# Twenty pieces of modulation weights, loaded from ScalarE's queue in place of SyncE's

## The chip, the core and the metric

The kernel runs on one core of a Trainium2 chip. A core has five engines that work side by side: TensorE (PE, matrix products into PSUM; its weight loads are shown apart as PEld), VectorE (DVE), ScalarE (ACT), GpSimd (POOL) and SyncE (SP), which computes nothing and issues transfers. Each engine takes its own list of instructions in order and waits at a semaphore until what an instruction needs is there. Transfers between the chip's main memory and the core's SBUF are moved by 16 DMA engines; SyncE, ScalarE and GpSimd can issue them, each on a queue of its own. An instruction of a queue that waits holds up everything behind it on that engine.

The metric is the device time of one execution in microseconds. The kernel before takes 3300.7 us (median of 3 runs, 3300.5 to 3307.68).

## The reference

Two transformer layers over 1024 latent tokens and 256 context tokens of width 1024. A vector `c` (and another, `c_ctx`, for the context) is turned into six rows a layer, which scale, shift and gate the layer's steps:

```
mod = silu(c) @ w_ada[l] + b_ada[l]        # w_ada: 2 x 1024 x 6144, float32
sh1, sc1, g1, sh2, sc2, g2 = split(mod, 6) # "the modulation"
h = x * (1.0 + sc1) + sh1
x = layer_norm(ALPHA * x + g1 * mixer(h), ...)
h = x * (1.0 + sc2) + sh2
x = layer_norm(ALPHA * x + g2 * mixture_of_experts(h), ...)
```

Layer 0's mixer is two kinds of attention side by side: window attention with grouped keys (8 heads) and two-dimensional neighbourhood attention (8 heads). Layer 1 has multi-head latent attention and differential attention. Both layers end in a mixture of 32 experts of which each token takes two.

## The kernel before

Float32 matrices are split into two float16 parts, high and low, and a product is three matrix products (`mm3`, lines 181 to 185: high by high, high by low, low by high). So each weight goes through the same steps: a load (SyncE), the high part by ScalarE (`high`, line 315, or line 374), the low part by VectorE (`low`, line 318, or line 375), products on TensorE.

The modulation (`ada`, lines 301 to 361) works in pieces of 512 columns, each in four chunks of 256 rows. A chunk is one load of 128 x 2 x 512 float32, 512 KB (`load`, line 311), a high part, a low part and four products into `ps_ada` (line 331). `ada` is called in two ways. Before the attention it runs four pieces to the end, with 8 tiles for the loads (`rbufs`) and a pool of PSUM of its own (`tps`). These four pieces, 16 loads, are what the first normalisation needs. The other twenty, 80 loads, make a background job (`bg`, line 793) without `tps`, with 3 tiles for the loads. A load of chunk n thus goes into the tile of chunk n - 3, and waits until its low part is made. The finished rows go to main memory (`mod_d`, line 339) and are read after the attention. The bias rows (`b_ada`, line 324) of the background job are issued by GpSimd.

Layer 0's attention (`attn_l0`) is six units: two of window attention with four heads each, four of neighbourhood attention with two heads each. While unit u is attended, `interleave` mixes in the projection of unit u + 1 (`proj_unit`), 16 chunks of the background job, and a table of biases. A unit's attention is a pipeline of six steps over its (tile, head) pairs: the scores on TensorE (lines 679 to 682, tile S), the maximum on VectorE (lines 702, 709), the exponentials on ScalarE (lines 706, 720, 723), the rounding to a high part on ScalarE (line 730), the low part on VectorE or GpSimd (line 737), the transpose of the probabilities of two heads by a DMA that SyncE issues (line 739), and the product with the values on TensorE (tile O, `mm3`'s lines 183 to 185). The projections end in a transpose too (line 628).

The program is written tile by tile; a scheduler puts the instructions of each engine in order, from what each needs and how long it takes them to be, and sets the semaphores. The order of the engines' lists is therefore the scheduler's, not the text's. Transfers take turns on eight semaphores (DMAHW0 to DMAHW7 below), whichever engine issues them.

Of the kernel before, what the change touches and what calls it, by code (L numbers as in the profile page):

```python
# [22 lines left out]
P = 128  # L23
# [145 lines left out]
class Kern:  # L169
# [131 lines left out]
    def ada(self, work, pool, pspool, rbufs, hbufs, bbufs, tps=None):  # L301


        nc = self.nc
        raws, parts, rows, sums = {}, {}, {}, {}

        def load(n):
            l, j = work[n // 4]
            cols, k = slice(j * 512, (j + 1) * 512), n % 4 * 2
            raws[n] = pool.tile([P, 2, 512], F32, name="adaraw", bufs=rbufs)  # L310
            nc.sync.dma_start(raws[n], self.i["w_ada"][l].rearrange("(k p) n -> p k n", p=P)[:, k:k + 2, cols])

        def high(n):
            parts[n] = pool.tile([P, 2, 2, 512], F16, name="adahl", bufs=hbufs)
            nc.scalar.activation(parts[n][:, 0], raws[n], AF.Copy, scale=SW)

        def low(n):
            nc.vector.scalar_tensor_tensor(parts[n][:, 1], raws[n], SW, parts[n][:, 0], op0=ALU.mult, op1=ALU.subtract)

        def products(n):  # L320
            if n % 4 == 0:
                l, j = work[n // 4]
                rows[n // 4] = pool.tile([2, 512], F32, name="ada_b", bufs=bbufs)
                (nc.gpsimd if tps is None else nc.sync).dma_start(
                    rows[n // 4], self.i["b_ada"][l:l + 1, j * 512:(j + 1) * 512].to_broadcast([2, 512]))
                sums[n // 4] = pspool.tile([P, 512], F32, name="ps_ada", tag="proj")
            ps = sums[n // 4]
            for q in range(2):
                k = n % 4 * 2 + q
                for a in range(2):  # L330
                    nc.tensor.matmul(ps, self.sc(k), parts[n][:, a, q],
                                     start=k + a == 0, stop=k == KD - 1 and a == 1)

        def end(c):
            (l, j), row, ps = work[c], rows[c], sums[c]
            for part in (ps[:2], ps[32:34]):
                nc.vector.scalar_tensor_tensor(row, part, 1.0 / (SA * SW), row, op0=ALU.mult, op1=ALU.add)
            if j >= 4:
                nc.sync.dma_start(self.mod_d[l, :, j * 512:(j + 1) * 512], row)
                return  # L340
            pt = (tps or pspool).tile([P, 4, 2], F32, name="ps_adat", tag="O" if tps else "proj")
            for q in range(4):
                nc.tensor.transpose(pt[:, q, :], row[:, q * P:(q + 1) * P], self.id32[:2, :2])
            dst = self.modTs[l][:, j // 2, (j % 2) * 4:(j % 2) * 4 + 4, :]
            if j < 2:
                nc.vector.tensor_scalar_mul(dst, pt, SA)
            else:
                nc.vector.tensor_scalar(dst, pt, 1.0, SA, op0=ALU.add, op1=ALU.mult)

        last = 4 * len(work) - 1  # L350
        for n in range(-1, last + 1):
            for m in range(0 if n < 0 else n + rbufs - 1, min(last, n + rbufs - 1) + 1):
                load(m)
            if n < last:
                high(n + 1)
            if n >= 0:
                low(n)
                products(n)
                if n % 4 == 3:
                    end(n // 4)  # L360
                yield
# [1737 lines left out]
```

## Time and profile before

| | |
|---|---|
| time, median of 3 runs | 3300.7 us |
| time of the profiled execution | 3299.66 us |
| its span, first to last instruction | 3297.6 us |
| TensorE busy | 2585.0 us (78%) |
| VectorE busy | 2610.6 us (79%) |
| ScalarE busy | 1968.3 us (60%) |
| GpSimd busy | 1017.3 us (31%) |
| transfers of SyncE's queue (q1) | 714.26 MB, 75.2% of 16 DMA engines' span |
| transfers of ScalarE's queue (q10) | 1.09 MB, 0.2% |
| TensorE's granted clock, mean | 0.900 |

"Busy" leaves out what a queue does: waiting, and issuing a transfer. A row named SPq or ACTq is the queue of SyncE or ScalarE; its duration is the issue, not the transfer. A row "A <- B: t, n, m" of the waits says that A was idle for t us in n places, the longest m, and that B's end released it.

### The profile page before, as it was taken

Reading aid. Unit: us, or ns where it says so; the run is one execution under the profiler, and the core shown is the slowest. Engines: PE = TensorE matmul, PEld = TensorE weight load, DVE = VectorE, ACT = ScalarE, POOL = GpSimd, SP = SyncE. Lnnn points to the kernel's source line nnn. Section 1 sums busy time; section 2 is a strip of 40 time slices with the busy share of each in tenths; the row PEclk is TensorE's granted clock in tenths of the full one; section 3 lists DMA queues with packets and bytes.
Section 4 is the critical chain, followed back from the end, with each engine's and each line's share of the span. In section 5 each row is a group of like instructions: output and inputs, shape, how many; then the busy total and the mean of one; then the engine's idle time right before and its main releaser. Section 6 shows DMA issues by size and latency. Waiting matters only on the chain. (4 is left out here: it accounts for less than half of the span.)

```text
span 3297.6 us, 74337 instructions
## 1 busy us (share of the span) xinstructions
PE 2585.0 (78%) x30127; PEld 1786.7 (54%) x30127; DVE 2610.6 (79%) x4429; ACT 1968.3 (60%) x2913; POOL 1017.3 (31%) x652
## 2 busy tenths in 40 slices
PE   6877888868579889997467778887868489888886
PEld 3555455534267777774245555555534267776653
DVE  6787777778897768887867776778877897889986
ACT  5567767653465566676345655566653465656664
POOL 0133233331342222221442332223221463233644
PEclk9999999979789989998689988998978689999998
DMA  7789999789768889998538999655558598999996
GB/s 246 158 179 192 194 205 188 166 209 214 255 248 336 323 326 364 365 379 334 201 101 152 174 158 181 125 99 99 122 125 213 171 345 325 356 367 381 385 377 247
DMA packets 879159, 790.05 MB, mean 240 GB/s; under 512 B 689397, under 2 KB 719365, under 8 KB 878805
## 3 DMA queue, kind: packets, MB, share of 16 engines
q1 hardware_dynamic: 846981, 714.26, 75.2%
q0 software_dynamic: 26336, 69.85, 6.5%
q8 instruction: 239, 3.92, 0.5%
q10 hardware_dynamic: 5488, 1.09, 0.2%
q14 instruction: 115, 0.94, 0.1%
HBM read 565.85 MB, written 64.55 MB: 191 GB/s over the span
## 5 line engine op out<-in xcount | busy, mean ns | idle before, releaser
L375 DVE SCALAR_TENSOR_TENSOR arena<-arena 128x2048 f16<-128x2048 f32 (+4 forms) x439 | 916.8, 2110 | 173.3 <-ACT arena L374 167.9
L374 ACT ACTIVATE arena<-arena 128x2048 f16<-128x2048 f32 (+4 forms) x439 | 749.5, 1726 | 317.8 <-DMA arena<-in_w_gate_up_dram 202.8
L1364 PE MATMUL pg<-arena 128*128 128x72 f16 (+4 forms) x4736 | 633.2, 210 | 105.9 <-DVE arena L1351 79.4
L1366 PE MATMUL pg<-arena 128*128 128x72 f16 (+4 forms) x4736 | 629.9, 210 | 26.0 <-DVE arena L375 21.1
L1365 PE MATMUL pg<-arena 128*128 128x72 f16 (+4 forms) x4736 | 630.8, 210 | 8.5 <-DVE arena L1351 7.0
L183 PEld LDWEIGHTS <-arena 128*128 128x128 f16 (+1 forms) x3488 | 346.5, 103 | 361.5 <-DMA arena<-arena 145.8
L1365 PEld LDWEIGHTS <-arena 128*128 128x128 f16 x4736 | 473.2, 102 | 68.1 <-issue 64.2
L1366 PEld LDWEIGHTS <-arena 128*128 128x128 f16 x4736 | 472.6, 102 | 51.1 <-DVE arena L375 33.0
L1364 PEld LDWEIGHTS <-arena 128*128 128x128 f16 x4736 | 473.2, 102 | 37.6 <-ACT arena L374 18.9
L184 PEld LDWEIGHTS <-arena 128*128 128x128 f16 (+1 forms) x3488 | 346.4, 103 | 198.2 <-issue 103.9
L1381 POOL DMA_INDIRECT y_d<-arena,rt_sidx x74 | 242.0, 3271 | 610.6 <-ACT arena L1394 302.4
L185 PEld LDWEIGHTS <-arena 128*128 128x128 f16 (+1 forms) x3488 | 346.6, 103 | 130.4 <-issue 22.9
L183 PE MATMUL O<-arena 128*128 128x64 f16 (+1 forms) x1744 | 229.9, 209 | 138.4 <-DMA arena<-arena 109.5
L184 PE MATMUL O<-arena 128*128 128x64 f16 (+1 forms) x1744 | 229.2, 208 | 0.0
L185 PE MATMUL O<-arena 128*128 128x64 f16 (+1 forms) x1744 | 229.0, 208 | 0.0
L1774 POOL TENSOR_TENSOR arena<-arena 128x1280 f16<-128x1280 f32 x57 | 151.6, 2660 | 245.9 <-issue 174.7
L1755 ACT ACTIVATE arena<-S,arena 128x1280 f32<-128x1280 f32 x128 | 169.1, 1321 | 91.5 <-DVE arena L1753 77.7
L1344 POOL DMA_INDIRECT arena<-h_d,rt_gidx x74 | 150.7, 2036 | 225.3 <-PE pt L1350 168.9
L1752 DVE TENSOR_REDUCE arena<-S 128x1 f32<-128x1280 f32 x128 | 189.5, 1481 | 29.0 <-PE S L185 17.5
L195 PE MATMUL py<-arena 128*72 128x512 f16 (+4 forms) x592 | 183.9, 392 | 21.2 <-ACT arena L1376 14.9
L197 PE MATMUL py<-arena 128*72 128x512 f16 (+4 forms) x592 | 182.3, 389 | 0.0
L199 PE MATMUL py<-arena 128*72 128x512 f16 (+4 forms) x592 | 179.7, 385 | 0.0
(393 smaller groups left out, 6254.0 us busy)
## 6 DMA issues: line engine op xcount, KB each, us to landing
arena<-in_w_gate_up_dram SPq DMA_DIRECT2D x256, 1024.0 KB
arena<-in_w_down_dram SPq DMA_DIRECT2D x128, 1024.0 KB
arena<-in_w_ada_dram SPq DMA_DIRECT2D x96, 512.0 KB
arena<-y_d SPq DMA_DIRECT2D x36, 512.0 KB
x_d<-arena POOLq DMA_DIRECT2D x18, 512.0 KB
h_d<-arena SPq DMA_DIRECT2D x18, 512.0 KB
arena<-x_d SPq DMA_DIRECT2D x18, 512.0 KB
arena<-in_x_dram SPq DMA_DIRECT2D x16, 512.0 KB
```

Source lines behind the costliest of these rows:

```text
L183: mm(ps, lh, rh, start=first, stop=False)
L184: mm(ps, lh, rl, start=False, stop=False)
L185: mm(ps, ll, rh, start=False, stop=last)
L195: mm(ps[:, o], lh, rh[:, o], start=first, stop=False)
L197: mm(ps[:, o], lh, rl[:, o], start=False, stop=False)
L374: nc.scalar.activation(wh, raw, AF.Copy, scale=scale)
L375: nc.vector.scalar_tensor_tensor(wl, raw, scale, wh, op0=ALU.mult, op1=ALU.subtract)
L1364: mm(pg[:, m, :n], wh, xh, start=k == 0 and m % 4 == 0, stop=False)
L1365: mm(pg[:, m, :n], wh, xl, start=False, stop=False)
L1366: mm(pg[:, m, :n], wl, xh, start=False, stop=k == 7 and m % 4 == 3)
L1381: self.K.nc.gpsimd.indirect_dma_start(out=self.K.y_d[self.l], out_offset=bass.IndirectOffsetOnAxis(ap=sidx, axis=0), in_=y[:n], in_offset= ...
L1752: nc.vector.reduce_max(mx[:, 0:1], S[:, :TOK], axis=AX.X)
```

## The change

The engine that issues line 311's load is chosen by whether the call has `tps`: with it (the 16 loads ahead of the attention) SyncE as before, without it (the 80 background loads) ScalarE.

```
@@ -308,7 +308,7 @@ def load(n)
             raws[n] = pool.tile([P, 2, 512], F32, name="adaraw", bufs=rbufs)
-            nc.sync.dma_start(raws[n], self.i["w_ada"][l].rearrange("(k p) n -> p k n", p=P)[:, k:k + 2, cols])
+            (nc.scalar if tps is None else nc.sync).dma_start(raws[n], self.i["w_ada"][l].rearrange("(k p) n -> p k n", p=P)[:, k:k + 2, cols])
```

The scheduler then orders all engines anew. The lists differ from about the end of the first normalisation to the end of the attention; later ones are the same. SyncE's list loses the 80 loads and ScalarE's gains them.

SyncE's list near the end of unit 0, before (`arena` is the SBUF space in which all tiles of this stage lie, 128x20x128 is a transpose of 20 blocks of 128 x 128, the brackets name the semaphores waited for):

```order
L739 DMA_TRANSPOSE arena<-arena 128x20x128 [waits DMAHW7_49,PE_49,Pool_49]
L311 DMA arena<-in_w_ada_dram 128x2x512 [waits DMAHW0_49,DVE_49]
L739 DMA_TRANSPOSE arena<-arena 128x16x128 [waits DMAHW1_49,DMAHW2_49,PE_49,Pool_49]
L628 DMA_TRANSPOSE arena<-arena 128x6x128 [waits DVE_49,Activation_49]
L311 DMA arena<-in_w_ada_dram 128x2x512 [waits DMAHW3_49,DVE_49]
L739 DMA_TRANSPOSE arena<-arena 128x16x128 [waits DMAHW4_49,DVE_49,PE_49]
L311 DMA arena<-in_w_ada_dram 128x2x512 [waits DMAHW6_49,DMAHW5_49,DVE_49]
L739 DMA_TRANSPOSE arena<-arena 128x8x128 [waits DVE_49,DMAHW7_49,PE_49,Pool_49]
```

The same place now:

```order
L739 DMA_TRANSPOSE arena<-arena 128x20x128 [waits DVE_49,DMAHW7_49,PE_49,Pool_49]
L739 DMA_TRANSPOSE arena<-arena 128x16x128 [waits DMAHW0_49,DVE_49,DMAHW1_49,PE_49,Pool_49]
L628 DMA_TRANSPOSE arena<-arena 128x6x128 [waits DMAHW2_49,DVE_49,Activation_49]
L739 DMA_TRANSPOSE arena<-arena 128x16x128 [waits DMAHW4_49,DVE_49,PE_49]
L739 DMA_TRANSPOSE arena<-arena 128x8x128 [waits DMAHW5_49,DVE_49,DMAHW7_49,PE_49,Pool_49]
```

The transposes stand in the same order with no load between them.

ScalarE's list in the middle of unit 1, before:

```order
L315 ACTIVATE arena<-arena 128x1024 [waits DMAHW3_49,PE_49]
L706 ACTIVATE arena<-S,arena 128x640 [waits DVE_49]
L706 ACTIVATE arena<-S,arena 128x640 [waits DVE_49,Pool_49]
L730 ACTIVATE arena<-arena 128x640 [waits DMAHW4_49,Activation_49]
L730 ACTIVATE arena<-arena 128x640 [waits Activation_49]
L763 ACTIVATE arena<-arena 128x4
L315 ACTIVATE arena<-arena 128x1024 [waits PE_49]
```

The same place now, where a load stands two instructions behind the high part of the chunk whose tile it takes:

```order
L315 ACTIVATE arena<-arena 128x1024 [waits DMAHW5_49,PE_49]
L730 ACTIVATE arena<-arena 128x640 [waits DMAHW4_49,Activation_49]
L311 DMA arena<-in_w_ada_dram 128x2x512 [waits DVE_49]
L706 ACTIVATE arena<-S,arena 128x640 [waits DVE_49,PE_49,Pool_49]
L706 ACTIVATE arena<-S,arena 128x640 [waits DVE_49,PE_49,Activation_49]
L730 ACTIVATE arena<-arena 128x640 [waits Activation_49]
L730 ACTIVATE arena<-arena 128x640 [waits DMAHW5_49,Activation_49]
L315 ACTIVATE arena<-arena 128x1024 [waits DMAHW6_49,PE_49]
```

The load waits for VectorE (DVE_49), and two exponentials and two roundings of the attention stand behind it.

## Rows read from the trace of the kernel before

**Rows 1.** The page's first line.

```profile
span 3297.6 us, 74337 instructions
```

**Rows 2.** Busy time by stretch; columns: stretch, length, engines in turn (instructions).

```profile
core 0: us, PE busy (x) PEld busy (x) DVE busy (x) ACT busy (x) POOL busy (x), PEclk, DMA share, GB/s
60.00:660.00 600.00, 489.87 (x4927) 309.63 (x4926) 459.73 (x1152) 400.90 (x888) 178.40 (x187) 0.95 0.86 183
```

**Rows 3.** Waits of TensorE and its weight loads, 60 to 660 us.

```profile
engine line waited for: us in total, times, longest us
PEld L183 <- DMA arena<-arena: 70.4, 37, 4.3
PE O L183 <- DMA arena<-arena: 56.7, 36, 3.9
...
PE S L679 <- ACT arena L706: 13.5, 15, 2.7
```

**Rows 4.** Waits of SyncE's queue, 60 to 660 us.

```profile
SPq L628 <- DVE arena L621: 59.7, 36, 6.6
SPq L739 <- DVE arena L737: 41.0, 29, 4.9
SPq L739 <- POOL arena L737: 39.2, 18, 4.7
SPq L311 <- DVE arena L318: 24.6, 16, 4.2
SPq L311 <- DVE arena L619: 19.7, 7, 6.2
```

**Rows 5.** Line 311, the load; ns shortest/median/longest, first and last start.

```profile
L311 SPq DMA_DIRECT2D arena<-in_w_ada_dram x96: 367/420/1472, 1.3 to 644.8; - x96
...
  ACT arena L315: 3.2, 2
```

**Rows 6.** Lines 739 and 628, the transposes, and who waited for line 739.

```profile
L739 SPq DMA_TRANSPOSE arena<-arena x80: 1231/3589/7596, 117.5 to 788.2; - x80
...
  PE O L183: 65.4, 41
...
L628 SPq DMA_TRANSPOSE arena<-arena x60: 1210/1212/2387, 73.2 to 658.0; - x60
```

**Rows 7.** Timeline of SyncE's queue, 190 to 199 us; start, duration.

```profile
191.03 0.39 SPq L311 DMA_DIRECT2D arena<-in_w_ada_dram  x1
191.89 4.98 SPq L739 DMA_TRANSPOSE arena<-arena  x1
...
197.37 2.68 SPq L739 DMA_TRANSPOSE arena<-arena  x1
```

**Rows 8.** Timeline of ScalarE at 31 us.

```profile
30.89 1.06 ACT L315 ACTIVATE arena<-arena 128x1024 f16<-128x1024 f32 x1 [0.67 <-PE ps_ada L331]
30.96 0.39 ACTq L555 DMA_DIRECT2D arena<-in_cos_dram  x1
```

**Rows 9.** Three small loads, as in rows 5: lines 284, 461 and 1626.

```profile
L284 SPq DMA_DIRECT2D arena<-in_c_dram x1: 449/449/449, 0.8 to 0.8; - x1
...
L461 ACTq DMA_DIRECT2D arena<-in_browmask_dram x1: 422/422/422, 0.8 to 0.8; - x1
...
L1626 ACTq DMA_DIRECT2D arena<-in_cos_dram x1: 374/374/374, 1715.8 to 1715.8; - x1
```

**Rows 10.** Timeline of ScalarE, two high parts.

```profile
249.08 1.06 ACT L315 ACTIVATE arena<-arena 128x1024 f16<-128x1024 f32 x1
...
310.76 1.06 ACT L315 ACTIVATE arena<-arena 128x1024 f16<-128x1024 f32 x1 [1.56 <-PE ps_ada L331]
```

**Rows 11.** Timeline of VectorE, the low parts of the same two chunks.

```profile
257.58 1.19 DVE L318 SCALAR_TENSOR_TENSOR arena<-arena 128x1024 f16<-128x1024 f32 x1
...
311.85 1.22 DVE L318 SCALAR_TENSOR_TENSOR arena<-arena 128x1024 f16<-128x1024 f32 x1 [0.68 <-ACT arena L315]
```

## The prediction

> **What bounds the kernel now.** I read the stretches first, since the change touches one stage alone. The profiled execution took 3299.7 us: its span of 3297.6 [rows 1] and 2.1 us around it; the median of the three runs is 3300.7, 1.0 more. The background loads are issued while layer 0's attention runs, from about 60 to 660 us. In these 600 us TensorE is busy for 489.87, VectorE for 459.73, ScalarE for 400.90, and the DMA engines have a share of 0.86 [rows 2]. The reader is to see that no engine is full: the three work between 67% and 82% of the stage, so it is held by the chain between them, not by one of them.
>
> The waits say which link of the chain comes last. TensorE's second product (probabilities by values, line 183 into tile O) waits 56.7 us in 36 pieces for a DMA that moves tile to tile, and its weight load waits 70.4 us for the same; its longest other wait with a named cause is 13.5 us, for ScalarE's exponentials [rows 3]. That DMA is the transpose of the probabilities, line 739, on SyncE's queue, where the loads stood too. So the first question is whether the loads make these transposes late.
>
> SyncE's own waits answer most of it: it stands 59.7 us at line 628 (the transpose of the projections) for VectorE, 41.0 and 39.2 us at line 739 for the low halves of the probabilities, and 24.6 and 19.7 us at line 311, the load, mostly because the tile to be loaded is not free yet [rows 4]. A queue that mostly waits for its inputs is no bottleneck. The load itself takes the queue 420 ns in the median, and ScalarE, which uses the data, waited for it only 3.2 us in 2 places [rows 5].
>
> **The change part by part.** (1) *80 issues leave SyncE.* There are 96 loads [rows 5], 16 of them before the stage, which stay; 80 x 0.42 = 34 us of issue and the 24.6 + 19.7 = 44 us of waiting at them leave that queue. What hides them: the 59.7 + 41.0 + 39.2 = 140 us which the queue waits for the transposes' inputs anyway. I take 0 for the issue time; if that cover were gone it would be a gain of up to 34 us.
>
> (2) *A transpose no longer stands behind a load in the same queue.* The 80 issues of line 739 take 3.6 us in the median, and TensorE waited for 41 of them [rows 6]. In SyncE's order 31 of the 80 stand directly behind a load. The price of one: a transpose of 20 blocks issued 0.5 us after a load took 4.98 us, one of the same size with no load ahead 2.68 [rows 7]: 2.3 us. At most 31 x 41/80 x 2.3 = 37 us come off TensorE's waits. At least nothing: the load's 512 KB still go through the same DMA engines, whose share is 0.86 [rows 2], and a load that ScalarE issues may now begin in the middle of a transpose, where SyncE could only put it between two. I take about a fifth, 8 us, near the lower end because of that share.
>
> The Trainium skill, page "DMA: Bandwidth & Descriptors", section "Issuing engines are not separate DMA queues", says that transfers interleave on the same 16 engines whoever issues them, and that a second issuer saves only the sequencer's issue time. By that page term (2) would be 0 and the forecast 8 us later, still no measurable change.
>
> (3) *80 issues come to ScalarE.* The nearest rows are its own few loads: 390 ns for line 555, 422 and 374 ns for two others [rows 8, 9], so 80 x 0.42 = 34 us. The engine need not lose them: at 30.89 a conversion of 1.06 us began, and the sequencer issued the load of line 555 beneath it, from 30.96 to 31.35 [rows 8]. A stage's mean instruction comes every 600/888 = 0.68 us [rows 2], longer than the issue. So I take 0; with nothing hidden it would be 34 us of ScalarE time.
>
> (4) *ScalarE now waits until the tile is free.* This is the wait the change adds. The load of chunk n needs VectorE's low half (line 318) of chunk n-3, which follows ScalarE's high half (line 315). Behind the waiting load stand the exponentials and roundings of the attention (lines 706, 720, 730), for which TensorE and the low halves wait. In one place the high half starts at 310.76 and the low half runs from 311.85 to 313.07, 2.3 us later; in a bad one the high half starts at 249.08 and the low half ends at 258.77, 9.7 us later [rows 10, 11]. In the new order of ScalarE the load stands 10 or more instructions behind that high half for 47 of 77 loads, 6 to 9 for 18, and 2 to 5 for 12. Two to five instructions are 1.4 to 3.4 us, so the 12 wait between 0 and 8 us; the others hardly. I take 12 x 1.5 = 18 us. ScalarE is idle for a third of the stage [rows 2], so I let a third of it through, hence 6 us longer, rounded down to 5 as some loads stand before a wait for VectorE that comes anyway. Bounds: 0, and the 44 us that SyncE waited at these loads [rows 4].
>
> (5) *The load starts later after the tile is free.* Its first use stands 7 to 42 ScalarE instructions behind it, and for 5 of 80 under 10. Seven are 4.8 us. In the kernel before, ScalarE waited twice for a load, 3.2 us in all [rows 5], and the longest wait for a DMA in the stage's rows is 3.9 us [rows 3]; I take 0, and at most 5 x 3.9 = 20 us.
>
> (6) *The rest of the order.* The waits of other engines, b_ada's rows on GpSimd and the transposes keep their queues; the order differs only between about 30 and 700 us, and the projections stand at nearly the same places on TensorE. 0.
>
> Sum: -8 + 5 = -3 us on 3299.7, or 3297.7 on the median: 3298.
>
> **The rivals.** *A: the transposes run free.* If loads and transposes on two queues overlap instead of standing in line, most of term (2) comes. For: TensorE's largest wait is this one [rows 3], and a transpose was seen stretched from 2.68 to 4.98 us [rows 7]. Against: share 0.86. Price: 60% of 37, 22 us, with nothing lost on ScalarE: 3278.
>
> *B, the other side: ScalarE's issue waits for SyncE's transpose.* If the two queues share what makes descriptors, a load that comes while a transpose is being issued stands on ScalarE until that is done. The transposes occupy SyncE for 60 x 1.21 + 80 x 3.59 = 360 us [rows 6] of the 715 between 73 and 788. A load at a random time then waits (60 x 1.21 x 1.21 + 80 x 3.59 x 3.59) / (2 x 715) = 0.78 us on the average: 63 us for 80, and with issue 97 us on an engine that has 199 us free. A quarter of that on the chain is 25 us: 3325. For: SyncE's load took up to 1.47 us [rows 5]. Against: no row of before has a load of ScalarE during a transpose. It decides when ScalarE's loads take over 0.9 us in the mean, twice rows 8 and 9. The Trainium skill, page "Perfetto Trace Analysis", section "DMA Instruction — HWDGE (DVE, Sync)", says this: descriptor generation is "locked for exclusive use" during an issue. No row of before shows it either way; the first loads of the kernel are a hint against it, issued on both queues at 0.8 us and done in 449 and 422 ns [rows 9].
>
> *C: the change does something else.* The list of each engine is rearranged, so a wait may move for no reason of the queues. TensorE is idle for 600 - 490 = 110 us of the stage [rows 2]; a tenth of it either way is 11 us: 3290 or 3312.
>
> **How the numbers follow.** About 0.3% (10 us) can be told from no change in this kernel. The forecast has 0.42: 0.34 within that bound, 0.05 faster, 0.03 slower. A has 0.28 (0.26 faster, 0.02 same), B 0.20, all slower, C 0.10 (0.04, 0.02, 0.04). Faster 0.35, same 0.38, slower 0.27. The forecast's own range is 3288 to 3308; the stated one reaches to A and B, 3274 to 3326.
>
> **What would show it.** Right: line 311 on ScalarE at 0.37 to 0.6 us, no new large wait of ScalarE for line 318, and TensorE's wait for the transposes between 45 and 60 us in the stage. A: line 739's median falls from 3.59 to under 3.0 us and TensorE's wait with it. B: line 311 in the mean over 0.9 us. Wrong altogether: the stage's end moves by more than 10 us while these rows stay, or a stage behind 800 us changes.

## The result, and the profile after

The changed kernel takes 3351.8 us (median of 4 runs, 3341.7 to 3352.7); the kernel before took 3301.1 beside it. The ratio is 1.0143, 95% interval 1.0125 to 1.0161: 51 us slower, where 3298 us and at most 3326 were forecast. The profiled execution took 3352.1 us; the first line of its page and its stretch from 60 to 660 us (columns as in [rows 2]):

```profile
span 3349.5 us, 74272 instructions
```

```profile
60.00:660.00 600.00, 467.63 (x4524) 293.97 (x4522) 415.36 (x1067) 364.22 (x808) 162.12 (x170) 0.91 0.79 168
```

Beside [rows 2] every engine is busy for less of these 600 us, and so are the DMA engines (0.79 for 0.86); the same work is stretched over a longer time. Line 739 last starts at 837.6 us for 788.2 [rows 6], so 49 of the 51 us are lost before that point, and the stages behind it keep their length within 3 us. The waits of TensorE and its weight loads, 60 to 660 us:

```profile
PEld L183 <- DMA arena<-arena: 102.5, 39, 6.3
PE O L183 <- DMA arena<-arena: 88.7, 37, 6.2
...
PE S L679 <- ACT arena L706: 10.8, 13, 1.8
```

TensorE waits for the transposed probabilities 32.0 us longer than in [rows 3], in about as many pieces; its wait for the exponentials did not grow. The waits of SyncE's queue:

```profile
SPq L739 <- DVE arena L737: 118.0, 38, 9.4
SPq L628 <- DVE arena L621: 74.8, 31, 5.8
SPq L739 <- POOL arena L737: 33.1, 17, 5.2
```

Where [rows 4] had waits at the load, SyncE now waits for the transposes' inputs instead: it comes earlier to an instruction that is not ready. The load and the two transposes (ns shortest/median/longest):

```profile
L311 ACTq DMA_DIRECT2D arena<-in_w_ada_dram x80: 374/374/788, 42.1 to 692.3; - x80
```

```profile
L739 SPq DMA_TRANSPOSE arena<-arena x80: 1231/3086/7302, 116.8 to 837.6; - x80
...
  PE O L183: 97.4, 43
```

```profile
L628 SPq DMA_TRANSPOSE arena<-arena x60: 1209/1216/3839, 69.0 to 706.1; - x60
```

The load costs ScalarE's queue 0.37 us. Line 739 occupies SyncE for less time than in [rows 6] (median 3.09 us for 3.59), and yet TensorE waits longer for it. That is the riddle of this case.

The bytes of the stage are now on two hardware queues. The DMA queues from 60 to 660 us (packets, MB, share of 16 engines); before, q1 alone had 82.5%:

```profile
q1 hardware_dynamic: 210716, 57.71, 53.0%
q10 hardware_dynamic: 19856, 38.28, 22.6%
```

### The profile page after: what moved, and what is told of

The parts are those of the page before. It is cut to its first block, busy times and chain, and to the rows that moved or that the text cites. A ratio compares the mean times of both kernels' runs of the same rounds, so it can differ in the third digit from the quotient of the medians.

```text
span 3349.5 us, 74272 instructions
## 1 busy us (share of the span) xinstructions
PE 2596.3 (78%) x30127; PEld 1797.9 (54%) x30127; DVE 2602.7 (78%) x4429; ACT 1967.4 (59%) x2913; POOL 1001.8 (30%) x652
## 5 line engine op out<-in xcount | busy, mean ns | idle before, releaser
L1381 POOL DMA_INDIRECT y_d<-arena,rt_sidx x74 | 227.7, 3077 | 616.7 <-ACT arena L1394 313.6
L183 PE MATMUL O<-arena 128*128 128x64 f16 (+1 forms) x1744 | 234.6, 210 | 175.2 <-DMA arena<-arena 143.9
L185 PE MATMUL O<-arena 128*128 128x64 f16 (+1 forms) x1744 | 234.9, 210 | 0.0
L184 PE MATMUL O<-arena 128*128 128x64 f16 (+1 forms) x1744 | 234.4, 210 | 0.0
```

Of the source, the lines that this page charges most:

```text
L183: mm(ps, lh, rh, start=first, stop=False)
L184: mm(ps, lh, rl, start=False, stop=False)
L185: mm(ps, ll, rh, start=False, stop=last)
L1381: self.K.nc.gpsimd.indirect_dma_start(out=self.K.y_d[self.l], out_offset=bass.IndirectOffsetOnAxis(ap=sidx, axis=0), in_=y[:n], in_offset= ...
```

## The experiments

Two things differ between the kernels: the queue of the loads, and the lists of all five engines, which the scheduler rearranged between about 30 and 700 us. To part them, the lists are held: the kernel takes the order of each engine's instructions from a table and chains them by ordering edges, which set the order and wait for nothing. In the traces of E1 and E2 below, each engine takes its instructions in the order of the kernel before and of the changed kernel, the loads apart.

**E1 and E2: one list, the other queue.** E1 has the lists of before and the loads on ScalarE, E2 the lists of after and the loads on SyncE. The edit, beside the queue at line 311 (`LISTS` has the instruction numbers of each engine in order; `...` stands for lines left out):

```diff
+    for eng, coded in LISTS.items():
...
+        for a, b in zip(names, names[1:]):
...
+            tc.add_manual_dep(by[b], a, no_sync, reason="order")
```

E1:

> Loads on ScalarE's queue as in the changed kernel, but every engine's list of layer 0's attention is held in the order of the kernel before by ordering edges; the 80 loads stand in ScalarE's list where the scheduler's common order of the kernel before had them. Theory 1 (the rearranged lists cost the 51 us, the queue costs nothing): 3301 us, 3291 to 3311, and TensorE's weight-load wait for the transposes stays near 70 us. Theory 2 (the queue itself costs: loads now overlap the transposes, or ScalarE stands at the loads): 3340 to 3352, with that wait near 105 us. Half of each: about 3325.

E2:

> The reverse: the loads are back on SyncE's queue, but every engine's list is held in the order of the changed kernel; the loads stand in SyncE's list where the scheduler's common order of the changed kernel had them. Theory 1 (lists): 3345 to 3365, slower than the kernel before by about all of the 51 us. Theory 2 (queue): 3301, 3291 to 3311. Half of each: about 3325. Together with the first run this is a table of two lists by two queues; if both effects are there and add, the four times must add up.

Measured: E1 3331.0 us, ratio 1.0089 (1.0067 to 1.0110), so +30. E2 3314.4 us, ratio 1.0037 (1.0016 to 1.0058), so +13. Neither time lies in a range that I had given for one theory alone; both effects are there. My theory 1, that the lists cost all of it, falls: the queue costs 30 us (22 to 36), the lists 13 (5 to 19). The two add to 43 of the 51; with the lists of after the queue costs 3351.8 - 3314.4 = 37. The 8 us between 43 and 51 are less than these intervals leave open, so it is not shown that the two effects do more together than apart. TensorE's wait, 60 to 700 us, in the kernel before, in E1 and in E2:

```profile
PE O L183 <- DMA arena<-arena: 60.3, 39, 3.9
```

```profile
PE O L183 <- DMA arena<-arena: 88.2, 41, 10.5
```

```profile
PE O L183 <- DMA arena<-arena: 56.3, 38, 4.3
```

The wait follows the queue, not the lists. Where E2's 13 us lie is not shown: its traced execution was one of its two fastest (3305.6 us), only 6 us above the traced one of the kernel before.

E1 can be laid on the kernel before one instruction upon another, since all lists are the same. Here is one transpose, first in the kernel before (timeline, SyncE and TensorE; start, duration):

```profile
207.92 3.70 SPq L739 DMA_TRANSPOSE arena<-arena  x1
211.73 0.51 SPq L311 DMA_DIRECT2D arena<-in_w_ada_dram  x1
...
213.34 0.20 PE L183 MATMUL O<-arena 128*128 128x64 f16 x1 [0.83 <-DMA arena<-arena]
```

and the same one in E1 (SyncE, ScalarE, TensorE):

```profile
209.99 3.42 SPq L739 DMA_TRANSPOSE arena<-arena  x1
...
212.37 0.37 ACTq L311 DMA_DIRECT2D arena<-in_w_ada_dram  x1
...
218.24 0.24 PE L183 MATMUL O<-arena 128*128 128x64 f16 x1 [4.76 <-DMA arena<-arena]
```

In one queue the load comes out 0.11 us after the transpose has been issued, behind it, and TensorE has its data 5.4 us after the transpose began. In E1 ScalarE issues the load while the transpose is still being issued, and TensorE has its data after 8.2 us. The transpose's own row did not grow with it (3.42 us for 3.70): a row of the queue ends with the issue, not with the landing.

Most of these cases cost 1 to 3 us. The worst of E1 shows best what happens: three loads were under way beside one transpose (two issued before it, one into it), and its issue took longer too, 14.91 us for 5.48 in the kernel before.

```profile
474.65 14.91 SPq L739 DMA_TRANSPOSE arena<-arena  x1
```

The queues of E1 from 477 to 480 us (q1 is SyncE's, q10 ScalarE's):

```profile
q10 hardware_dynamic: 430, 0.84, 82.9%
q1 hardware_dynamic: 164, 0.03, 13.8%
```

In these 3 us 430 of the loads' packets passed, some 2 KB each, and only 164 of SyncE's queue, 0.03 MB in all.

So theory C (contention): a load on a second queue shares the DMA engines with a transpose that is under way, while in the one queue it waits behind it. Its rival B: ScalarE itself stands at the loads. To test C over all 80 transposes I took from each trace the moment at which a transpose's semaphore had its last of 16 marks (it has landed), and the time from the end of its issue to that moment (the tail, a mean in the table), apart for those into whose issue a load started ("entered") and for the rest:

| kernel | total us | TensorE's wait at line 183, us | transposes entered | tail of these, us | tail of the rest, us |
|---|---|---|---|---|---|
| before | 3301 | 60.3 | 0 | - | 2.29 |
| E1 | 3331 | 88.2 | 31 | 4.41 | 2.41 |
| E2 | 3314 | 56.3 | 0 | - | 2.26 |
| after | 3352 | 90.7 | 23 | 4.41 | 2.35 |

(the wait is TensorE's second product, 60 to 700 us). From SyncE no load can start inside, since the queue issues one thing after the other. A transpose that was not entered lands nearly as before. It is not that long transposes are entered more often: the 31 that are entered in E1 have a tail of 2.25 us in the kernel before.

The wait is not all that grew. From 60 us to the last transpose of line 739 the three kernels run the same 5,700 or so matrix products (the kernel before, E1, the changed kernel; columns as in [rows 2]):

```profile
60.00:788.20 728.20, 580.84 (x5717) 359.46 (x5716) 558.99 (x1373) 471.21 (x1046) 214.92 (x226) 0.93 0.87 188
```

```profile
60.00:822.30 762.30, 593.09 (x5710) 365.41 (x5709) 557.56 (x1370) 472.79 (x1046) 217.23 (x226) 0.91 0.84 180
```

```profile
60.00:837.60 777.60, 602.04 (x5717) 372.03 (x5715) 552.35 (x1374) 470.57 (x1047) 218.20 (x226) 0.89 0.81 176
```

TensorE is busy for 12 us longer in E1 and for 21 us longer in the changed kernel, at a mean granted clock of 0.91 and 0.89 for 0.93 (means over stretches at 2.4 and at 1.2 GHz). The wait grew by 28 and 30 us, the stretch by 34 and 49. So a part of the loss is TensorE running the same products at a lower clock. That the longer waits brought the clock down was not tested, and how much of it lies on the chain stays open.

**E3 and E4: the issues stay, the bytes go.** The lists of before are held; the load is cut to 32 of 512 columns (the edit of E3; E4 has `nc.sync` alone in the second line):

```diff
+            w = slice(j * 512, j * 512 + 32) if tps is None and n > 2 else cols
+            (nc.scalar if tps is None else nc.sync).dma_start(raws[n][:, :, :w.stop - w.start], ...[:, k:k + 2, w])
```

E3, on ScalarE:

> The lists of the kernel before are held and the loads stand on ScalarE's queue, as in the first run, but 77 of the 80 background loads bring only 32 of 512 columns (32 KB for 512). The modulation is computed from old weights, so what follows the stage may route tokens differently; the comparison is by the last transpose of line 739 (788.2 us in the kernel before, 822.3 in the first run) and by the total only if the later stages keep their length. Theory C (contention: loads on a second queue mix with the transposes on the same 16 DMA engines, so the transposes land later): the delay is gone, last transpose at 788 or earlier, to about 755. Theory B (ScalarE stands at the loads, whatever they move): still 815 to 825.

E4, on SyncE:

> The same small loads on SyncE's queue, lists of the kernel before held: the control for the run beside it. Both theories: last transpose of line 739 at 788 or earlier, since no transpose stands behind a large load any more; how much earlier is the gain that the prediction's term 2 bounded at 37 us. Theory C: the run with the small loads on ScalarE ends its stage within 6 us of this one. Theory B: it ends 25 to 35 us later than this one.

Measured: the later stages did change length (3535 and 3528 us in all), so the stage decides. The transposes (line 740 here), E3 and then E4:

```profile
L740 SPq DMA_TRANSPOSE arena<-arena x80: 1231/3074/6973, 119.0 to 768.5; - x80
```

```profile
L740 SPq DMA_TRANSPOSE arena<-arena x80: 1231/3089/7541, 117.7 to 758.9; - x80
```

The last one starts at 768.5 us in E3, for 822.3 with the full loads in E1: the delay goes with the bytes, although ScalarE issues and waits as often. 26 transposes were still entered by a small load, and their tails are 2.40 us for 2.26 of the rest. E3 ends 10 us behind E4, more than C's 6 and far from B's 25 to 35. E4 also sizes term 2 of the prediction: without the loads' bytes the last transpose starts 29 us earlier than in the kernel before, for the at most 37 of that term. Each of these times is from one traced execution.

**E5 and E6: the dose.** All data arrive, split by columns over both queues, C columns by ScalarE:

```diff
+                nc.scalar.dma_start(raws[n][:, :, :C], src[:, :, :C])
+                nc.sync.dma_start(raws[n][:, :, C:], src[:, :, C:])
```

E5, C = 32:

> Each background load is split by columns: 32 of 512 by ScalarE's queue, 480 by SyncE's, each at the place that the load has in the first run and in the kernel before; lists held, all data arrive. ScalarE issues and waits 80 times as in the first run, but 15/16 of the bytes go through SyncE's queue. Theory C: 3301 to 3311 us. Theory B: 3325 to 3337 us.

E6, C = 256:

> As the run beside it, but split in halves: 256 columns by ScalarE's queue, 256 by SyncE's. Theory C: the cost follows the bytes on the second queue, so about half of the first run's 30 us: 3311 to 3321 us. Theory B: it follows the issues and waits, 3325 to 3337 us, as the first run.

Measured: E5 3302.0 us, ratio 1.0011 (0.9990 to 1.0031); E6 3316.6, ratio 1.0079 (1.0050 to 1.0107). With 1/16, 1/2 and all of the bytes on ScalarE's queue the cost by the medians is 2, 16 and 30 us, each against the runs of the kernel before beside it (3300.2, 3300.2 and 3301.3). By the ratios it is 4 (-3 to 10), 26 (17 to 35) and 29 us (22 to 36): the cost grows with the bytes, but that half of them cost half is not shown. The number of transposes entered is nearly the same in the three, 31, 30 and 31, and ScalarE issues as often; the tails of the transposes that were entered are 2.57, 3.56 and 4.41 us. (These tails overstate the growth somewhat: the traced executions of E5 and E6 are among their fastest, E1's is its slowest.) B falls: ScalarE's part is within E5's cost, not told from none.

The second queue's packets are also as many in all three, only smaller; 60 to 700 us, E5, E6 and E1:

```profile
q10 hardware_dynamic: 21488, 2.59, 2.9%
```

```profile
q10 hardware_dynamic: 21488, 20.71, 11.2%
```

```profile
q10 hardware_dynamic: 21488, 41.42, 21.3%
```

So it is not the number of packets on the second queue that costs, but what they carry. Whether the two transfers meet in the DMA engines themselves or in the memory behind them is not told apart here.

TensorE's wait in E5 and in E6:

```profile
PE O L183 <- DMA arena<-arena: 62.9, 39, 3.5
```

```profile
PE O L183 <- DMA arena<-arena: 71.4, 36, 5.0
```

**E7 and E8: another place in the one queue.** Is it the place in SyncE's queue that counts, loads ahead of transposes? Only SyncE's list is changed. E7 at one place (the order of SyncE):

```
-L311 DMA arena_58<-in_w_ada_dram 128x2x512
-L739 DMA_TRANSPOSE arena_58<-arena_58 128x20x128 x2
+L739 DMA_TRANSPOSE arena_58<-arena_58 128x20x128
+L311 DMA arena_58<-in_w_ada_dram 128x2x512
+L739 DMA_TRANSPOSE arena_58<-arena_58 128x20x128
```

> All loads on SyncE's queue and all other lists as in the kernel before; in SyncE's list alone the 34 loads that stand directly ahead of a transpose of line 739 go directly behind it. If the bytes ahead of a transpose are what costs, and a load behind a transpose in the same queue costs it nothing, TensorE's waits for the transposes fall below the 60.3 us (second product) of the kernel before, and the total falls by up to the 29 us that the small loads on SyncE gave: 3280 to 3298 us. If a load behind one transpose only delays the next one, nothing is gained: 3298 to 3306. If the later loads make ScalarE wait for its data (line 315): over 3306.

E8, at one place:

```
-L311 DMA arena_58<-in_w_ada_dram 128x2x512
 L739 DMA_TRANSPOSE arena_58<-arena_58 128x20x128 x2
-L311 DMA arena_58<-in_w_ada_dram 128x2x512
+L311 DMA arena_58<-in_w_ada_dram 128x2x512 x2
```

> As the run beside it, but each load goes to the first place, at most three transposes or other transfers later, behind which SyncE's queue waited at least 3 us in the trace of the kernel before (24 of 80 loads move; for the others no such gap follows, or they stand at one). If loads cost only the transposes that follow at once, this is the faster of the two: 3278 to 3296 us. If the place of a load in the one queue does not matter: 3298 to 3306. If late loads starve line 315: over 3306.

Measured: E7 3299.0 us, ratio 1.0003 (0.9993 to 1.0014): nothing. E8 3296.8 us, ratio 0.9988 (0.9976 to 1.0000): at most 0.24% faster, within what counts here as no change. TensorE's wait is 62.7 us in E7 and 56.5 in E8, for 60.3. At the places tried, the place of a load in the one queue hardly matters; a load moved from one transpose stands before another. In E7 line 315 also waits longer for its data (11.5 us for 3.2), which may hide a small gain.

**E9 and E10: another place in the second queue.** The loads are on ScalarE, and only its list is changed. E9 against E1, at one place (order of ScalarE):

```
-L311 DMA arena<-in_w_ada_dram 128x2x512
 L706 ACTIVATE arena<-S,arena 128x640 x2
-L730 ACTIVATE arena<-arena 128x640 x2
+L730 ACTIVATE arena<-arena 128x640
+L311 DMA arena<-in_w_ada_dram 128x2x512
+L730 ACTIVATE arena<-arena 128x640
```

> Loads on ScalarE's queue and lists of the kernel before held, as in the first run, but in ScalarE's list each load (65 of 80; 15 would come too near their use) goes to the next place directly behind a rounding (line 730) of an even head, after which no transpose is due until the odd head's softmax has run. Theory C, in the form that a load hurts when it starts while a transpose is under way and not when it started before: fewer loads start inside a transpose, so 3301 to 3318 us, clearly below the first run's 3331. If only the bytes on a second queue count, wherever they stand: 3325 to 3335.

E10 moves the loads behind the rounding of an odd head instead:

> The opposite of the run beside it: each load (68 of 80) goes four instructions behind the next rounding (line 730) of an odd head, 2 to 3 us later, when the transpose of that pair is as a rule being issued. Theory C in that form: more loads start inside a transpose, 3335 to 3360 us, above the first run. If only the bytes on a second queue count: 3325 to 3335, as the run beside it.

Measured: E9 3318.1 us, ratio 1.0048 (1.0033 to 1.0062); E10 3353.8 us, ratio 1.0147 (1.0126 to 1.0169). With the same bytes on the same second queue the place alone makes 36 us, where the two places tried in the one queue are 2 us apart and at most 4 from the kernel before. TensorE's wait in E9 and in E10:

```profile
PE O L183 <- DMA arena<-arena: 79.9, 35, 6.5
```

```profile
PE O L183 <- DMA arena<-arena: 106.0, 36, 12.1
```

The times came as expected (E9's at the upper end of its range), but not for the reason I gave. E9 did not keep the loads out: 36 transposes were entered, against 31 in E1 and 37 in E10 (by 43, 35 and 51 loads). Nor was it late data: line 315 waited 4.5 us for its loads in E9 and not at all in E10. What differs is how much each hurts: tails of 4.00, 4.41 and 4.55 us, and of the rest 2.37, 2.41 and 2.61. The time from issue to landing, summed over the 80 transposes, puts them in the order of their times: 456 us before, 509 in E9, 530 in E1, 569 in E10, for totals of 3300, 3318, 3331 and 3354. It does so for one set of lists only: the changed kernel, with its own lists, has 491 us and 3352. Counting the meetings is not enough; why those of E9 are milder (earlier in the transpose, fewer at once) I did not test.

## Why the prediction was wrong

*Step 1* (80 issues leave SyncE: 0) held. SyncE waits for inputs instead, 118.0 us for VectorE at line 739.

*Step 2* (-8 us, between 0 and -37) is where it failed, and in the sentence on its lower end: "At least nothing". I saw that a load "may now begin in the middle of a transpose" and used it only to shrink a gain. It was the main effect: with the lists held the term is +30 us (E1), with the new lists +37, for -8. [Rows 7] did show what a load costs a transpose beside it, 2.3 us; I counted only the meetings that go and none that come. In hindsight, E1's 31 transposes entered, at about 2 us each (tail 4.41 for 2.41) and half of that on the chain as in the prediction, give 31 us. That it fits is in part luck: the same sum gives 24 us for the changed kernel's 23, where the queue cost 37, and it leaves out TensorE's lower clock.

*Step 3* (ScalarE's issue hidden) held: 0.374 us each, under running activations, and E5 has the same issues for 2 us in all. *Step 4* (+5 us for ScalarE's waits at the loads) was not seen apart from that: E5, with the old lists, bounds steps 3 and 4 together at 0.31%, 10 us. *Step 5* held; no wait of ScalarE for a load is left at line 315. (Its bound used 3.9 us as the longest wait in [rows 3], which shows one of 4.3; the sum does not change.)

*Step 6* (the rest of the order: 0) was wrong by 13 us (E2, 5 to 19), a little over rival C's 11. E2's wait for the transposes is even below that of the kernel before, so the cost lies in other places of the rearranged lists; which, was not settled. So of the 51 us the queue has 30 to 37 and the lists about 13; the few that are left over are within the intervals.

*Rival A* fell, though its sign came: line 739's median went from 3.59 to 3.09 us, near the 3.0 that I had named. I had taken the issue of a transpose for its landing; in E1 the median fell too, and the tail behind it grew. *Rival B* had the right sign and the wrong cause: line 311 takes 0.374 us on ScalarE in the median and 0.79 at the longest, not over 0.9 in the mean, so ScalarE's issues did not stand behind SyncE's transposes, 23 of which they entered. The range reached 3326 for B alone; a cost of both queues on the DMA engines, with its own price, was not among the rivals.

The Trainium skill, page "DMA: Bandwidth & Descriptors", section "Issuing engines are not separate DMA queues", was read as making term 2 zero. Its sentence, that transfers interleave on the same 16 engines, agrees with the traces: from 477 to 480 us of E1 packets of both queues passed, 430 and 164. That nothing is lost by it was my conclusion, and E1's 30 us speak against it. The Trainium skill, same page, section "Queues, rings and completion order", says that an engine takes turns between its queues, a packet at a time, and that the descriptors of one queue are taken in order. By these two together a load on a second queue would take turns with a transpose that it would have followed; no run here shows the turns one by one.

## What to carry to other kernels

A queue is also an order: here a prefetch that nobody waited for, issued behind a transfer on the critical path, left that transfer alone, and a second queue took that protection away. Before moving bulk loads off the queue of small urgent transfers, count how many would start inside one and price each by what the tail grows, here about 2 us for 512 KB and 0.1 to 0.3 for 32 KB. Such a sum gives the sign and the rough size; the place in the second queue alone moved the time by 36 us. Judge a transfer by when its reader starts, not by its row in the issuing queue, which got shorter here while the kernel got slower.

## What the runs showed that was not expected

- The issue of a transpose can itself take longer beside another queue's loads: 14.91 us for 5.48, with three loads beside it in E1.
- In one queue two other places of the loads made no difference that can be told (0.9988 and 1.0003 of the time), though without their bytes the stage is 29 us shorter.
- The same matrix products took TensorE 21 us longer in the changed kernel, at a lower granted clock, though nothing about them was changed.
- The scheduler's rearrangement after an edit of one line cost 13 us with the queue unchanged; holding the lists is what made the queue's part visible.
